# A streaming encoder on one core: layer B's q, k and v of three chunks by seven half-size products (Strassen's scheme) for eight

## Chip, core and metric

The kernel runs on one core of one Trainium2 chip. The metric is the device time of the execution in microseconds; the time before is the median of three runs. TensorE, VectorE, ScalarE and GpSimd work side by side, each through its own queue in order; SyncE issues most of the DMAs.

## What is computed

A two-layer trunk over 2048 tokens of width 1024, all in float32. The part that the change touches is layer B's input: from the stream x after layer A, the shared keys and values and the queries.

```python
kv_in = rms_norm(x, kv_norm)
k_all, v_all = jnp.split(kv_in @ w_kv, 2, axis=-1)
k_sh = rms_norm(split_heads(k_all), k_norm)
v_sh = split_heads(v_all)
h = rms_norm(x, b_norm[j])
q, z = jnp.split(h @ b_w_in[j], 2, axis=-1)
q = rms_norm(split_heads(q), b_q_norm[j])
o = stick_breaking_attention(q, k_sh, v_sh)
```

So q, k and v are each a product of (tokens x 1024) with (1024 x 1024), a row scale 1/rms per token, and for q and k a norm per head of 64.

## The kernel before

**Stages.** The tokens are cut into four chunks of 512 (`s`, 0 to 3). A first program part runs per chunk 22 steps: four pairs z and u of layer A's input (`run_z`, `run_u`), four of its output projection (`run_o`), four of the gated embedding (`run_g`, b = 0 to 3), and six of q, k, v (`run_kvq`, two column halves b of 512 for each kind). Then a second part sweeps the attention over all chunks, with layer B's z, output projection and embedding interleaved. That second part is not touched.

**Precision.** Every float32 operand of a matmul is split into a rounded high part and the remainder (a "pair", `[P, 2, 512]`), and a product is three matmuls: high x high, low x high, high x low. The high part is written by ScalarE (`split` L215, `load_w` L106 or with a gain L112), the low part, the difference, by VectorE or GpSimd (L216, L108, L113).

**The step q, k, v.** `run_kvq` (L526) takes token blocks j of 128 in pairs (`j0` 0 and 2); for each, eight blocks kt of the contraction times three matmuls into two PSUM banks (L536: token block stationary, 512 weight columns moving). That makes 2 x 2 x 8 x 2 x 3 = 192 matmuls a kind and 576 a chunk. `token_major` scales the bank by the row scale on ScalarE (L617 for q, k; L579 for v). For q and k, `keyed` squares (L619), reduces (L621), takes the root by two GpSimd operations (L79, L80), `normed` multiplies (L629), and `finish` transposes four tiles on TensorE (L638) and stores the pair to DRAM (`qd`, `kd`). For v, the rows are shifted by one token by DMA, subtracted on GpSimd (L609), halved and stored (`vd`).

**Weights.** `load_w` brings a block of 128 x 512 into `raw` (pools `io`, 10 buffers shared with other uses, and `wraw`, 3), and makes the pair in `wpair`, twelve buffers in two pools. The main loop at the end calls the load of step i + 1 ahead of the run of step i. A q, k or v step needs eight such blocks, 48 a chunk, each used for both `j0`. Weights of the second part are halved once and stored (`keep`), one or two per step in steps 8 to 21.

**Order.** The program is recorded in the order of the code, and a scheduler then places instructions on each engine, so an engine's row of instructions mixes several steps. What it made of both programs is shown under the change.

**Buffers named below.** PSUM: six banks `psd` for products (four and two, `dense()`), two `pst` for transposes. SBUF: `act`, 18 pairs (x, m, x1, x2); `t2` with tags `tmp` (8), `qn` (5), `ub` and `us` (2 each, of `run_u`'s pooling), `t4` (3).

**The embedding stage.** `run_g(s, b)` makes two tiles o = 2b and 2b + 1 of the stream: sigmoid (L506), multiply (L508), add (L509), halve into x2 (L215, L216), and a running sum of squares `acc` (L521, L524) which gives the row scale r2.

## Time and profile before

| | us |
|---|---|
| runs: median (lowest, highest) | 2769.08 (2768.56, 2769.49) |
| profiled execution: span of its instructions | 2765.4 |
| q, k, v stage of chunk 0, 1, 2, 3 | 143.2, 143.2, 143.7, 139.4 |
| embedding stage (four steps) of chunk 1, 2, 3 | 54.8, 56.5, 55.9 |

The profile gives the profiled execution's span, from its first to its last instruction; of time around the span it shows none, and the runs' median lies 3.7 us above it. A stage here is the stretch from its first matmul to the next stage's first. In a row of a group, the numbers after the bar are the time in which the group was busy, the mean ns of one instruction, and the idle time of the engine just ahead of them with what ended it. A matmul's own duration overlaps with the next one's; its pitch is read from a run of many. "128x512" is partitions x elements.

### The profile page before, as it was taken

Reading aid. Unit: us, or ns where it says so; the run is one execution under the profiler, and the core shown is the slowest. Engines: PE = TensorE matmul, PEld = TensorE weight load, DVE = VectorE, ACT = ScalarE, POOL = GpSimd, SP = SyncE. Lnnn points to the kernel's source line nnn. Section 1 sums busy time; section 2 is a strip of 40 time slices with the busy share of each in tenths; the row PEclk is TensorE's granted clock in tenths of the full one; section 3 lists DMA queues with packets and bytes.
Section 4 is the critical chain, followed back from the end, with each engine's and each line's share of the span. In section 5 each row is a group of like instructions: output and inputs, shape, how many; then the busy total and the mean of one; then the engine's idle time right before and its main releaser. Section 6 shows DMA issues by size and latency. Waiting matters only on the chain. (4 is left out here: it accounts for less than half of the span.)

```text
span 2765.4 us, 39537 instructions
## 1 busy us (share of the span) xinstructions
PE 2725.7 (99%) x13715; PEld 2260.4 (82%) x13715; DVE 1956.0 (71%) x2573; ACT 1385.5 (50%) x2801; POOL 873.7 (32%) x695
## 2 busy tenths in 40 slices
PE   9999999999999999999999999999999999999999
PEld 7888888888888888888888888887887778888877
DVE  6766535655357544565499999999999988996632
ACT  5444532445234542345356566666666655664521
POOL 2574338642475325753121111111110011112220
PEclk9999999999999999999999999999999999999999
DMA  8664696747946479445678565555555566668765
GB/s 293 236 196 171 218 325 204 225 148 253 347 148 227 163 249 318 136 145 170 191 254 278 180 217 170 169 161 178 169 159 162 159 200 200 188 204 264 249 209 160
DMA packets 335835, 573.21 MB, mean 207 GB/s; under 512 B 32462, under 2 KB 166638, under 8 KB 335636
## 3 DMA queue, kind: packets, MB, share of 16 engines
q1 hardware_dynamic: 330186, 563.03, 63.5%
q10 hardware_dynamic: 5450, 7.66, 0.9%
q8 instruction: 108, 1.77, 0.3%
q14 instruction: 91, 0.75, 0.1%
HBM read 430.01 MB, written 132.19 MB: 203 GB/s over the span
## 5 line engine op out<-in xcount | busy, mean ns | idle before, releaser
L844 ACT CAST at<-psa 128x512 fp32r<-128x512 f32 (+3 forms) x640 | 334.1, 522 | 478.4 <-PE psa L841 459.6
L536 PE MATMUL psd<-wpair,x 128*128 128x512 f32 x2304 | 544.0, 393 | 0.0
L828 DVE TENSOR_TENSOR_SCAN pp<-kap,pp,zeros 128x512 f32<-128x512 f32 x384 | 512.9, 1336 | 3.1 <-ACT kap L820 2.4
L536 PEld LDWEIGHTS psd<-wpair,x 128*128 128x128 f32 x2304 | 428.2, 188 | 86.2
L845 DVE TENSOR_TENSOR at<-psa,at 128x512 fp32r<-128x512 f32 (+3 forms) x640 | 381.0, 596 | 88.0 <-ACT at L844 84.9
L841 PE MATMUL psa<-ident,pp 128*128 128x128 f32 x2176 | 347.0, 275 | 17.2 <-DVE at L845 15.5
L820 ACT ACTIVATE kap<-psl 128x512 f32<-128x512 f32 (+3 forms) x640 | 344.9, 539 | 15.1 <-PE psl L817 12.0
L841 PEld LDWEIGHTS psa<-ident,pp 128*128 128x128 f32 x2176 | 262.9, 140 | 93.0 <-DVE at L845 38.8
L816 PE MATMUL psl<-kk,qa 128*128 128x512 f32 (+3 forms) x640 | 281.4, 440 | 0.0
L854 PE MATMUL pso<-at,vv 128*128 128x512 f32 (+3 forms) x640 | 235.1, 367 | 0.0
L817 PE MATMUL psl<-kk,qb 128*128 128x512 f32 (+3 forms) x640 | 233.0, 364 | 0.0
L853 PE MATMUL pso<-at,vv 128*128 128x512 f32 (+3 forms) x640 | 232.7, 364 | 0.0
L825 DVE TENSOR_TENSOR_SCAN pp<-kap,ahead 128x128 f32<-128x128 f32 (+3 forms) x256 | 219.8, 859 | 5.8 <-ACT kap L820 4.1
L131 PE MATMUL psd<-xp,wpair 128*128 128x512 f32 x512 | 201.9, 395 | 1.3 <-ACT xp L269 0.8
L132 PE MATMUL psd<-xp,wpair 128*128 128x512 f32 x512 | 200.5, 392 | 0.0
L133 PE MATMUL psd<-xp,wpair 128*128 128x512 f32 x512 | 200.1, 391 | 0.0
L113 DVE SCALAR_TENSOR_TENSOR wpair<-wraw,gains,wpair 128x512 fp32r<-128x512 f32 x192 | 169.7, 905 | 36.8 <-ACT wpair L112 36.1
L923 POOL TENSOR_TENSOR zr<-zr,sgz 128x512 f32<-128x512 f32 x32 | 58.8, 1836 | 368.2 <-ACT sgz L922 311.3
L112 ACT ACTIVATE wpair<-wraw,gains 128x512 fp32r<-128x512 f32 x192 | 135.0, 720 | 59.0 <-PE psd L536 32.3
L108 POOL TENSOR_TENSOR wpair<-wraw,wpair 128x512 fp32r<-128x512 f32 x99 | 145.5, 1485 | 59.7 <-ACT wpair L106 59.7
L853 PEld LDWEIGHTS pso<-at,vv 128*128 128x128 f32 x640 | 120.2, 188 | 26.9 <-ACT at L844 0.2
L854 PEld LDWEIGHTS pso<-at,vv 128*128 128x128 f32 x640 | 120.3, 188 | 25.9
(211 smaller groups left out, 5402.4 us busy)
## 6 DMA issues: line engine op xcount, KB each, us to landing
kk<-kd SPq DMA_DIRECT2D x320, 128.0 KB
vv<-vd SPq DMA_DIRECT2D x160, 256.0 KB
wraw<-in_w_kv_dram SPq DMA_DIRECT2D x128, 256.0 KB
wpair<-wzd SPq DMA_DIRECT2D x64, 512.0 KB
wpair<-wod SPq DMA_DIRECT2D x64, 512.0 KB
wpair<-wgd SPq DMA_DIRECT2D x64, 512.0 KB
wpair<-wu SPq DMA_DIRECT2D x48, 512.0 KB
wpair<-wi SPq DMA_DIRECT2D x36, 512.0 KB
```

Of the source, the lines that this page charges most:

```text
L131: T.matmul(ps, wst(units, kt, 0, c0), acts[kt][:, 0], start=(begin and kt == order[0]), stop=False)
L536: T.matmul(pss2[i], ck["x2"][kt][:, xh, tk], wst(ws, kt, wh, 0, W5), start=(kt == 0 and xh == 0 and wh == 0), stop=(kt == KT - 1 and wh == 1))
L816: T.matmul(ps[:, :w], qa[:, qs], kk[:, :w], start=True, stop=False)
L817: T.matmul(ps[:, :w], qb[:, qs], kk[:, :w], start=False, stop=True)
L820: A.activation(out=kp[:, r0:], in_=ps[:, :w], func=AF.Sigmoid, scale=-1.0)
L825: V.tensor_tensor_scan(out=pp[:, r0:][:, ::-1], data0=kp[:, r0:][:, ::-1], data1=ahead[:, r0:][:, ::-1], initial=1.0, op0=ALU.mult, op1=AL ...
L828: V.tensor_tensor_scan(out=pp[:, ::-1], data0=kp[:, ::-1], data1=zeros.to_broadcast([P, W5]), initial=st["carry"][j], op0=ALU.mult, op1=AL ...
L841: T.transpose(pt[:, j * P : (j + 1) * P], pp[:, r0 + kt * P : r0 + (kt + 1) * P], ident)
L844: A.copy(out=at[:, 0, cs], in_=pt[:, cs])
L845: V.tensor_tensor(out=at[:, 1, cs], in0=pt[:, cs], in1=f(at[:, 0, cs]), op=ALU.subtract)
L853: T.matmul(po[:, cs], vv[:, kt, :], at[:, 0, cs], start=(st["diag"] and kt == 0), stop=False)
L854: T.matmul(po[:, cs], vv[:, kt, :], at[:, 1, cs], start=False, stop=(st["last"] and kt == 3))
```

## The change

For chunks 1 to 3 (chunk 0 stays with `run_kvq`), the 1024 x 1024 product of each kind is cut into halves of the contraction (x2 tiles 0 to 3 and 4 to 7), of the tokens (256 each) and of the columns (512 each), and computed with seven products of half-size blocks and sums (Winograd's form of Strassen's scheme). With token and contraction halves A11, A12, A21, A22 of the stream and B11 to B22 of the weights:

- S1 = A21 + A22, S2 = S1 - A11 (tile `sum12`, its pair `s12`); S3 = A11 - A21, S4 = A12 - S2 (`sum34`, `s34`); made in `run_g`, b = 2 and 3, by half-width adds on GpSimd or VectorE and halved into eight more pairs
- T1 = B12 - B11, T2 = B22 - T1, T3 = B22 - B12, T4 = B21 - T2; made once by `combine`, twelve calls (three kinds, four blocks each) in chunk 0's q, k, v steps and chunk 1's steps 10 to 15, and stored in DRAM (`wtd`)
- the seven steps of a kind, in order, with the PSUM pair that each accumulates in: "11" (b), "21" (a), 2 (b, onto 11), 1 (c), 3 (b, onto 2), 4 (b, onto 3), "22" (c, onto 1). Each is 4 x 2 x 3 = 24 matmuls. Between them ScalarE copies out p1 (b after 11, tag `ub`), u2 (b after 2, tag `us`) and u3 (b after 3, tag `ub`), and VectorE adds them to what is in a or c; block 4's sum is copied by ScalarE

A step loads four weight blocks, 28 a kind and 84 a chunk; those of 1, 2, 3 and 4 come from `wtd` and need no gain. Loads run two steps ahead within these steps. The row scale goes into the square and the norm instead of a separate scaling. Transposes and stores go by pairs of token blocks. The next chunk's x is brought in and transposed in v's steps alone. The stored weights of the second part are spread otherwise over the steps.

```diff
+    def load_block(pools, src, base, gain, kind, block):
...
+            if block in (1, 2, 3, 4):
+                nc.sync.dma_start(out=raw, in_=wtd[kind, block, k])
+                A.copy(out=pr[:, 0, 0], in_=raw)
+                state["w"] += 1
+                (G if state["w"] % 2 else V).tensor_tensor(out=pr[:, 1, 0], in0=raw, in1=f(pr[:, 0, 0]),
+                                                           op=ALU.subtract)
+            else:
...
+                A.activation(out=pr[:, 0, 0], in_=raw, func=AF.Identity, scale=g)
+                V.scalar_tensor_tensor(out=pr[:, 1, 0], in0=raw, scalar=g, in1=f(pr[:, 0, 0]),
+                                       op0=ALU.mult, op1=ALU.subtract)
...
+            if b == 3:
+                u, v = held.pop()
+                halves("s12", u, V)
+            for k, t in zip((2 * b - 4, 2 * b - 3), ts):
+                lo = ck["t"][k]
+                eng = G if b == 2 else V
+                if k == 3:
+                    halves("s34", v, G)
+                    v = held.pop()
+                u = t2.tile([P, W5], F32, tag="ub", name="sum12", bufs=2)
+                w = t2.tile([P, W5], F32, tag="us", name="sum34", bufs=2)
+                eng.tensor_tensor(out=u[:, :H], in0=lo[:, H:], in1=t[:, H:], op=ALU.add)
+                eng.tensor_tensor(out=u[:, H:], in0=u[:, :H], in1=lo[:, :H], op=ALU.subtract)
+                G.tensor_tensor(out=w[:, :H], in0=lo[:, :H], in1=lo[:, H:], op=ALU.subtract)
+                G.tensor_tensor(out=w[:, H:], in0=t[:, :H], in1=u[:, H:], op=ALU.subtract)
...
+        def run_seven(s, kind, block, ws):
...
+            left, bank, c0 = {
+                "11": (x2[:4], "b", 0), "21": (x2[4:], "a", 0), 2: (s12, "b", 2 * P), 1: (s12, "c", 0),
+                3: (s34, "b", 0), 4: (x2[4:], "b", 2 * P), "22": (s34, "c", 2 * P)}[block]
+            begin = block in ("11", "21", 1)
+            if begin:
+                ck[bank] = [dense(), dense()]
+            pss2 = ck[bank]
+            for k in range(4):
+                for i in range(2):
+                    tk = slice(c0 + i * P, c0 + (i + 1) * P)
+                    for xh, wh in ((0, 0), (1, 0), (0, 1)):
+                        T.matmul(pss2[i], left[k][:, xh, tk], ws[k][:, wh, 0, :],
...
+            def kept(tag, nm, j0):
...
+                    t = t2.tile([P, W5], F32, tag=tag, name=nm, bufs=2)
...
+                        A.copy(out=t, in_=pss2[i])
...
+            if block == "11":
+                ck["p1"] = kept("ub", "p1", 0)
+            elif block == "21":
+                final(ck["a"], ck["p1"], 0, 0)
+            elif block == 2:
+                ck["u2"] = kept("us", "u2", 0)
+            elif block == 3:
+                final(ck["c"], kept("ub", "u3", 2), 1, 2)
+            elif block == 4:
+                final(ck["b"], None, 0, 2)
+            elif block == "22":
+                final(ck["c"], ck["u2"], 1, 0)
...
+            s, step = (0, i) if i < 22 else divmod(i - 22 + 37, 37)
+            ahead_of = 3 if s and step >= 15 else 2
```

**Where instructions stand, first place: VectorE where chunk 2's embedding stage ends and its q begins.** `sg2`, `tx2`, `x2` are the last two tiles of the embedding, `wpair` weight blocks. Before:

```order
L508 TENSOR_TENSOR sg2_8586<-psd_8524,sg2_8586 128x512
L508 TENSOR_TENSOR sg2_8587<-psd_8525,sg2_8587 128x512
L509 TENSOR_TENSOR tx2_8518<-sg2_8586,tx2_8518 128x512
L509 TENSOR_TENSOR tx2_8520<-sg2_8587,tx2_8520 128x512
L113 SCALAR_TENSOR_TENSOR wpair_8633<-wraw_8634,gains_101,wpair_8633 128x512
L216 TENSOR_TENSOR x2_8595<-tx2_8518,x2_8595 128x512
L216 TENSOR_TENSOR x2_8600<-tx2_8520,x2_8600 128x512
L621 TENSOR_REDUCE ssq_8722<-sqq_8720 128x8
```

After the change, from the same four instructions (sg2, sg2, tx2, tx2) on:

```order
L583 TENSOR_TENSOR sum12_9043<-tx2_8663,tx2_8946 128x256
L140 TENSOR_TENSOR wpair_9097<-wraw_9098,wpair_9097 128x512
L247 TENSOR_TENSOR x2_9023<-tx2_8946,x2_9023 128x512
L247 TENSOR_TENSOR x2_9028<-tx2_8948,x2_9028 128x512
L584 TENSOR_TENSOR sum12_9043<-sum12_9043,tx2_8663 128x256
L247 TENSOR_TENSOR s12_9040<-sum12_8894,s12_9040 128x512
L247 TENSOR_TENSOR s12_9049<-sum12_9043,s12_9049 128x512
L583 TENSOR_TENSOR sum12_9055<-tx2_8665,tx2_8948 128x256
L140 TENSOR_TENSOR wpair_9137<-wraw_9138,wpair_9137 128x512
L584 TENSOR_TENSOR sum12_9055<-sum12_9055,tx2_8665 128x256
L140 TENSOR_TENSOR wpair_9147<-wraw_9148,wpair_9147 128x512
L247 TENSOR_TENSOR s12_9061<-sum12_9055,s12_9061 128x512
```

Three instructions between tx2 and the next stage's work have become twelve.

**Second place: ScalarE in the same stretch, somewhat later.** `p1` is the copy of block 11's banks. Before:

```order
L215 CAST x2_8595<-tx2_8518 128x512
L521 ACTIVATE sq_8604<-tx2_8518 128x512
L215 CAST x2_8600<-tx2_8520 128x512
L521 ACTIVATE sq_8608<-tx2_8520 128x512
L548 COPY ss2_8713<-pst_8708 128x4
L617 ACTIVATE qs_8718<-psd_8658,r2all_103 128x512
```

After:

```order
L246 CAST s34_9052<-sum34_8895 128x512
L138 CAST wpair_9137<-wraw_9138 128x512
L682 COPY p1_9128<-psd_9102 128x512
L138 CAST wpair_9142<-wraw_9143 128x512
L138 CAST wpair_9147<-wraw_9148 128x512
L246 CAST s12_9061<-sum12_9055 128x512
L246 CAST s34_9064<-sum34_9044 128x512
L246 CAST s34_9067<-sum34_9056 128x512
L682 COPY p1_9130<-psd_9103 128x512
L138 CAST wpair_9218<-wraw_9219 128x512
```

The two p1 copies now stand among the halving of the sums, and the second waits for VectorE to be done with sum12_9055, whose buffer it takes.

**Third place: TensorE from block 3 to block 4 of chunk 2's q** (banks 9102 and 9103 are b; 9586 is the bank of k's block 11). Before, two token pairs of q follow each other in different banks:

```order
L536 MATMUL psd_8658<-wpair_8513,x2_8600 128x512 x3
L536 MATMUL psd_8659<-wpair_8513,x2_8600 128x512 x3
L545 MATMUL pst_8708<-ones_65,acc_8610 128x1 x4
L536 MATMUL psd_8742<-wpair_8478,x2_8195 128x512 x3
L536 MATMUL psd_8743<-wpair_8478,x2_8195 128x512 x3
```

After:

```order
L663 MATMUL psd_9102<-wpair_9233,s34_9067 128x512 x3
L663 MATMUL psd_9103<-wpair_9233,s34_9067 128x512 x3
L663 MATMUL psd_9586<-wpair_9410,x2_8617 128x512
L663 MATMUL psd_9102<-wpair_9266,x2_8865 128x512 x3
L663 MATMUL psd_9103<-wpair_9266,x2_8865 128x512 x3
```

Block 4 follows block 3 in the same two banks, with one matmul of another product between them.

## Prediction

> **What bounds the kernel now.** I read the page first, then the busy time of the engines stage by stage, then the matmul pitch, then the groups of the engines that feed TensorE.

> ```profile
> span 2765.4 us, 39537 instructions
> PE 2725.7 (99%) x13715; PEld 2260.4 (82%) x13715; DVE 1956.0 (71%) x2573; ACT 1385.5 (50%) x2801; POOL 873.7 (32%) x695
> PEclk9999999999999999999999999999999999999999
> ```

> TensorE is busy for 99% of the span at full granted clock, so time leaves the kernel only where matmuls leave it, or where the clock or the pitch changes. The stages that the change touches, by their stretches (the q, k, v stages of chunks 1, 2 and 3, and the gated-embedding stage before chunk 2's):

> ```profile
> core 0: us, PE busy (x) PEld busy (x) DVE busy (x) ACT busy (x) POOL busy (x), PEclk, DMA share, GB/s
> 563.30:706.50 143.20, 143.16 (x682) 118.69 (x681) 71.97 (x110) 75.35 (x149) 49.05 (x44) 1.00 0.63 209
> 837.80:894.30 56.50, 55.42 (x246) 45.33 (x245) 42.73 (x47) 29.15 (x55) 33.82 (x22) 1.00 0.73 244
> 894.30:1038.00 143.70, 143.38 (x682) 118.58 (x681) 72.62 (x106) 72.97 (x141) 49.17 (x44) 1.00 0.63 207
> 1225.40:1364.80 139.40, 139.36 (x651) 115.49 (x649) 65.73 (x95) 62.79 (x101) 44.32 (x40) 1.00 0.50 164
> ```

> In all three q, k, v stages TensorE never pauses, while VectorE and ScalarE are half idle and the DMA engines a third idle. That idle half is what the change spends. One unbroken run of these matmuls gives the pitch:

> ```profile
> 1351.75 13.08 PE L536 MATMUL psd<-wpair,x 128*128 128x512 f32 x57
> ```

> 13.08 us for 57 is 0.2295 us each.

> **The change, part by part.**

> *Matmuls removed.* A chunk has 576 of them now and 7 x 24 x 3 = 504 afterwards, 72 fewer in each of three chunks. 216 x 0.2295 = **-49.6 us**. Transposes are as many as before (only paired otherwise), so nothing else leaves TensorE. [...]

> *The start of each Strassen stage.* Here a wait is added. The first product (block 11) accumulates in the banks psd_9102 and psd_9103; block 21 follows in others; then block 2 accumulates onto the first banks again, so p1, the copy of the first product, must have been taken out. The two p1 tiles take the two "ub" buffers, and these hold the last two operand sums, sum12_9043 and sum12_9055. The second p1 copy therefore stands on ScalarE behind VectorE's s12_9061, the sixteenth VectorE instruction that is left when the embedding stage's matmuls end. VectorE's speed there, and TensorE's:

> ```profile
> 894.09 1.27 DVE L508 TENSOR_TENSOR sg<-psd,sg 128x512 f32<-128x512 f32 x2
> 895.29 1.28 DVE L509 TENSOR_TENSOR tx<-sg,tx 128x512 f32<-128x512 f32 x2
> 894.33 9.00 PE L536 MATMUL psd<-wpair,x 128*128 128x512 f32 x39
> L113 DVE SCALAR_TENSOR_TENSOR wpair<-wraw,gains,wpair 128x512 fp32r<-128x512 f32 x12 | 15.8, 1338 | 1.7 <-ACT wpair L112 1.7
> L216 DVE TENSOR_TENSOR x<-tx,x 128x512 fp32r<-128x512 f32 x8 | 9.6, 1234 | 0.0
> L509 DVE TENSOR_TENSOR tx<-sg,tx 128x512 f32<-128x512 f32 x8 | 6.2, 818 | 0.0
> L508 DVE TENSOR_TENSOR sg<-psd,sg 128x512 f32<-128x512 f32 x8 | 5.1, 679 | 0.0
> L108 DVE TENSOR_TENSOR wpair<-wraw,wpair 128x512 fp32r<-128x512 f32 x4 | 4.5, 1125 | 6.5 <-ACT wpair L106 6.5
> L211 ACT COPY rbx<-pst 128x512 f32<-128x512 f32 x3 | 1.7, 579 | 0.0
> ```

> The first three rows are of the time around 894.33, where the stage starts; the next five are means over 837.8 to 907. VectorE work with both sources in SBUF is slow there because GpSimd works at the same time: the halving of a weight takes 1.338 against 0.773 in the stage after it (row below), the one from PSUM stays at 0.679. From 894.33, VectorE has the two sg behind it at +1.0; two tx (0.82) +2.7; then, in the order of the changed program, half-width sum (half of 1.23) +3.3; weight 1.13 +4.4; two x2 +6.9; sum +7.5; two s12 +10.0; sum +10.6; weight +11.7; sum +12.3; weight +13.5; s12_9061 +14.7; and the p1 copy (0.58) +15.3. TensorE reaches psd_9103 after 51 matmuls, +11.7. It waits 3.6 us; what stands behind it on TensorE is everything, on ScalarE behind the copy the weights of block 3, which have 11 us. Bounds: if GpSimd left VectorE alone (0.64 for each as in the first two rows, 0.77 for a weight, half of that for a sum), s12_9061 is done at +9 and nothing waits; if all its two-source work took 1.34, at +17.1, and the wait is 6.0. I take 3.6, since GpSimd gets twelve half-width adds, two halvings and weights just there: **+10.8 us** for three chunks (0 to 18).

> *Bank taken twice in a row.* Block 4 accumulates onto the banks of block 3, from which u3 has just to be copied; in q and k one matmul of the next product stands between, in v of chunks 1 and 2 transposes. The last product on the first bank starts 0.92 us before block 4 could, takes 0.39, so the copy can run from -0.5 to +0.1; half of another ScalarE instruction (0.72, row below) ahead of it makes +0.4. Nine times about 0.5: **+4.5 us** (0 if the filler covers it; 14 if two instructions stand ahead).

> *Feeding the products.* A chunk loads 84 weight blocks for 48. Order and rows, per chunk:

> ```profile
> L113 DVE SCALAR_TENSOR_TENSOR wpair<-wraw,gains,wpair 128x512 fp32r<-128x512 f32 x37 | 27.8, 773 | 6.0 <-ACT wpair L112 6.0
> L112 ACT ACTIVATE wpair<-wraw,gains 128x512 fp32r<-128x512 f32 x37 | 26.0, 720 | 9.0 <-PE psd L536 7.3 <-PE psd L133 1.5 <-DMA kd<-hl 0.2
> L629 DVE TENSOR_TENSOR qn<-qs,rq 128x512 f32<-128x512 f32 x16 | 11.0, 690 | 11.8 <-POOL rq L80 11.7
> DMA packets 17582, 29.92 MB, mean 209 GB/s; under 512 B 1564, under 2 KB 9500, under 8 KB 17572
> ```

> (of 563.3 to 706.5.) VectorE had 72 us of work there. In the changed program's stage it has 23 differences of combined weights (x 1.125 = 25.9), 18 evictions from PSUM (x 0.68 = 12.2), sums and their halves (about 6), and nine fewer weights with gain (-7.0): 109 us in a stage of about 132. ScalarE: 75.4, and 45 casts of weights (at most 0.72, so 28 to 32) for nine weights with gain (-6.5), and some ten more casts of sums and stored weights (6): about 105. DMA: 0.63 x 143.2 = 90 us for 29.9 MB, and 42 more loads of 0.26 MB make about 33 more: 123. All three fit beside TensorE, with two blocks (11 us) of weights ahead as cushion, so this would cost nothing; but three in-order queues at 80 to 93% do not mesh perfectly, and I take 1.5 us a chunk, **+4.5 us** (0 to 42; the upper end is the second rival).

> *Made once.* The twelve combinations stand beside chunk 0's q, k, v, whose VectorE and GpSimd are as idle as chunk 1's above (hidden), and beside chunk 1's output and embedding stages. There each adds two VectorE and two GpSimd operations, and with the sums GpSimd goes from 34 of 56 us to about 55: the start of chunk 1's stage then comes later. **+3 us** (0 to 8). Moving the stored halves of other weights (the "kept" loads) from chunk 3 into chunks 1 and 2's stages is within the 123 and 105 above. The entry into attention gets v's heads 0 to 7 later by some 16 us (three blocks less follow them), but their first use is eight steps in: nothing (0 to 8).

> Sum: -49.6 + 10.8 + 4.5 + 4.5 + 3.0 = -26.8. The profiled span of 2765.4 becomes 2738.6; the runs shown lie 3.7 us above the span (median 2769.08), which I carry: **2742.3 us**.

> **The rivals.**

> *Everything hides.* If the p1 copies come in time and the bank copies fit under the filler, the gain is nearly whole: 2769.1 - 49.6 + 3 = 2722 to 2730. For it speaks that VectorE's two pairs at 894 ran at 0.64 even with GpSimd's weights just before; against it that GpSimd will now be busy without a break there.

> *VectorE becomes the bound* (the other side). The 109 us take VectorE's undisturbed durations. If GpSimd's 22 new differences slow all two-source work as in the embedding stage, 28 weights cost 0.565 more and 16 norms perhaps 0.4 more: 131. VectorE also waits now 11.8 us for GpSimd's rq (row of qn); with GpSimd at twice the work, 23.6: 155, less the cushion of eight weights (9): 146 against 143.2 in chunks 1 and 2; chunk 3 has 65.7 now, so 139 against 139.4. It decides when VectorE's work and waits pass 152 us a stage; with two or three more waits of the same kind (+4 a chunk) the whole is 2769 + 3 + 3 + 0 + 12 = 2787. A part of the way gives 2758 to 2772.

> *The clock drops in the pause.* At the start of the program the matmuls ran at 0.43 us until 11 us, then at 0.23:

> ```profile
> 8.82 0.63 PE L133 MATMUL psd<-xp,wpair 128*128 128x512 f32 x1
> 9.25 0.63 PE L132 MATMUL psd<-xp,wpair 128*128 128x512 f32 x1
> 11.20 0.40 PE L132 MATMUL psd<-xp,wpair 128*128 128x512 f32 x1
> 11.44 0.39 PE L133 MATMUL psd<-xp,wpair 128*128 128x512 f32 x1
> PE psao L986 <- DVE sg L980: 7.2, 4, 2.4
> 2762.00:2765.40 3.40, 0.00 (x0) 0.00 (x0) 0.00 (x0) 0.12 (x1) 0.00 (x0) 0.52 0.27 77
> ```

> and once TensorE had ended, the clock was granted at 0.52. From the first dense matmul (7.4) to full speed took 3.6 us, at about half pace, so a pause that lowers the clock costs 1.8 more, 5.4 for three: 2748. No pause inside the span lowered it, but the longest that TensorE spent on one wait was 2.4 us (the row of its waits, last number). [...]

> **How the numbers follow.** Forecast (three pauses, small leaks, 2730 to 2757) 0.52; everything hides 0.14; the clock drops 0.07; a late entry into attention or a backlog from chunk 1's combinations, 2750 or so, 0.05; VectorE bound 0.22, of which 0.05 ends below 2763, 0.08 within 0.2% of 2769 and 0.09 above. 0.2% (5.5 us) is about what a measurement of this kernel can tell from no change. So faster 0.83, same 0.08, slower 0.09. The range goes from 2722 (everything hides) to 2772, which leaves out some 0.05 below and 0.10 above.

> **What would show it.** Right: in the three stages 504 matmuls at 0.2295, one pause of 3 to 4 us in TensorE 11 to 16 us after each stage's start, released by ScalarE's p1 copy, and stages of about 131 us (127 in chunk 3). Wrong, if that pause is absent and the stage takes 127 us; if the pauses lie evenly over q and k and end with weights from VectorE (the bound moved); if granted clock falls below 1.00 after the pause; or if other stages grow.

## The result, and the profile after

| | before | after |
|---|---|---|
| median of 4 runs, us | 2768.82 (2768.47 to 2769.49) | 2916.38 (2914.14 to 2921.65) |
| profiled execution, us | span 2765.4 | span 2919.9, time 2921.65 |

The ratio is 1.0536, 95% interval 1.0521 to 1.0551: the change makes the kernel 148 us slower. 2742.3 was forecast, and the range ended at 2772.

The head of the page after, to be read against the three lines of before: span, busy time of the engines, granted clock in 40 slices.

```profile
span 2919.9 us, 40205 instructions
PE 2740.6 (94%) x13499; PEld 2256.2 (77%) x13499; DVE 2115.6 (72%) x2711; ACT 1480.6 (51%) x2957; POOL 1063.5 (36%) x839
PEclk9999999989999999999999999999999999999999
```

The 216 matmuls are gone (13715 to 13499), and still TensorE is busy 14.9 us longer. Its idle time (span less busy) went from 39.7 to 179.3 us: 139.6 of the 154.5 us are pauses. The rest is pace: 14.9 us more busy time with 49.6 us of matmuls removed means that the others took 64.5 us more. Most of that is the clock: in the stretches in which it was halved TensorE was busy for 111.7 us in all. Matmuls of 512 columns started 0.43 us apart there (1257.82 to 1260.38, clock 0.50) and 0.23 us apart at full clock (1261.37 to 1264.32), so about half of the 111.7, some 56 us by estimate, is lost pace. The rest of the 64.5 was not traced.

The stages of after: q, k, v of chunk 0; then in turn what lies between two such stages and the q, k, v of chunks 1, 2 and 3. The first number behind the stretch is its length, the next TensorE's busy time.

```profile
core 0: us, PE busy (x) PEld busy (x) DVE busy (x) ACT busy (x) POOL busy (x), PEclk, DMA share, GB/s
236.20:396.00 159.80, 146.31 (x681) 119.13 (x680) 75.67 (x114) 80.93 (x142) 58.96 (x50) 0.99 0.67 221
396.00:600.90 204.90, 193.72 (x829) 157.93 (x828) 116.39 (x130) 76.68 (x135) 133.58 (x109) 0.97 0.76 255
600.90:779.20 178.30, 138.73 (x609) 111.92 (x608) 125.69 (x152) 100.60 (x197) 104.50 (x85) 0.89 0.73 241
779.20:974.50 195.30, 189.64 (x829) 156.31 (x829) 109.24 (x128) 68.19 (x129) 130.05 (x107) 0.98 0.76 250
974.50:1149.00 174.50, 144.95 (x609) 115.79 (x609) 116.62 (x144) 97.00 (x189) 94.35 (x79) 0.88 0.68 219
1149.00:1348.50 199.50, 191.27 (x830) 157.08 (x828) 106.63 (x128) 69.20 (x129) 132.66 (x109) 0.97 0.69 224
1348.50:1509.80 161.30, 135.82 (x580) 109.63 (x579) 107.78 (x131) 83.88 (x142) 87.20 (x71) 0.89 0.59 187
```

Before, the three stages of the seven products took 143.2, 143.7 and 139.4 us with TensorE never idle; now 178.3, 174.5 and 161.3 at a mean clock of 0.89. Chunk 0's stage, whose matmuls did not change, takes 159.8. The stretches between, 204.9, 195.3 and 199.5, were these:

```profile
376.90:563.30 186.40, 186.40 (x830) 154.42 (x830) 103.80 (x122) 66.65 (x124) 122.72 (x99) 1.00 0.73 241
706.30:894.30 188.00, 186.92 (x829) 154.27 (x828) 104.83 (x124) 65.44 (x123) 121.36 (x98) 1.00 0.70 235
1037.90:1225.40 187.50, 186.95 (x830) 154.28 (x829) 106.64 (x120) 65.21 (x122) 118.99 (x95) 1.00 0.65 211
```

What TensorE waited for in chunk 2's stage of after (total us, times, longest one):

```profile
PE pst L800 <- DVE qn L790: 7.7, 5, 2.2
PE pst L800 <- DVE hl L812: 6.0, 1, 6.0
PE psd L663 <- ACT p L682: 6.0, 2, 4.7
PE psd L663 <- ACT u L680: 5.3, 2, 3.3
PE psd L663 <- DVE wpair L147: 3.1, 1, 3.1
```

The two longest items are the transposes of q and k (L800). One such pair of tiles, in time; start, duration, and in brackets the wait and its releaser:

```profile
1037.25 0.68 DVE L700 TENSOR_TENSOR qs<-psd,u 128x512 f32<-128x512 f32 x1
1039.28 1.30 POOL L140 TENSOR_TENSOR wpair<-wraw,wpair 128x512 fp32r<-128x512 f32 x1 [2.50 <-ACT wpair L138]
1041.26 1.64 POOL L83 TENSOR_TENSOR rq<-ms,neghalf 128x8 f32<-128x8 f32 x1
1042.93 0.75 DVE L790 SCALAR_TENSOR_TENSOR qn<-qs,r2all,rq 128x512 f32<-128x512 f32 x1 [1.22 <-POOL rq L83]
1043.83 1.64 POOL L83 TENSOR_TENSOR rq<-ms,neghalf 128x8 f32<-128x8 f32 x1
1045.50 1.74 DVE L790 SCALAR_TENSOR_TENSOR qn<-qs,r2all,rq 128x512 f32<-128x512 f32 x1 [1.81 <-POOL rq L83]
1047.76 1.40 DVE L812 SCALAR_TENSOR_TENSOR hl<-pst,gqk,hl 128x512 fp32r<-128x512 f32 x2
1048.56 1.12 PE L800 MATMUL pst<-ident,qn 128*128 128x128 f32 x4 [6.00 <-DVE hl L812]
```

From the eviction (qs, 1037.25) to the end of the second qn (1047.24) it takes 10.0 us: a weight's difference stands on GpSimd ahead of the mean and root, the two roots follow each other there, and VectorE waits in order for each. The eviction hl of the transposes before stands on VectorE behind both qn, so their bank comes free only then. TensorE reaches these transposes one block of 24 matmuls (5.5 us) after the products.

The clock around that pause, in stretches of 3.4 us (last three columns: granted clock, DMA share, GB/s):

```profile
1042.10:1045.50 3.40, 0.46 (x2) 0.03 (x1) 0.75 (x1) 1.46 (x3) 3.23 (x4) 1.00 0.41 131
1045.50:1048.90 3.40, 0.34 (x2) 0.35 (x3) 3.40 (x4) 0.00 (x0) 1.19 (x1) 0.50 0.24 76
1048.90:1052.30 3.40, 3.40 (x13) 2.91 (x12) 1.61 (x3) 1.19 (x2) 1.27 (x1) 0.50 0.92 310
1052.30:1055.70 3.40, 3.40 (x16) 2.81 (x16) 1.96 (x3) 2.49 (x6) 0.58 (x2) 1.00 0.92 293
```

The pause of 6 us halves the clock for two stretches, and the second of them is full of work at half pace.

### The profile page after: what moved, and what is told of

Its sections match the earlier page's. It is cut to its first block, busy times and chain, and to the rows that moved or that the text cites. A ratio compares the mean times of both kernels' runs of the same rounds, so it can differ in the third digit from the quotient of the medians.

```text
span 2919.9 us, 40205 instructions
## 1 busy us (share of the span) xinstructions
PE 2740.6 (94%) x13499; PEld 2256.2 (77%) x13499; DVE 2115.6 (72%) x2711; ACT 1480.6 (51%) x2957; POOL 1063.5 (36%) x839
## 5 line engine op out<-in xcount | busy, mean ns | idle before, releaser
L1057 PE MATMUL psa<-ident,pp 128*128 128x128 f32 x2176 | 346.9, 274 | 18.1 <-DVE at L1061 16.5
L1036 ACT ACTIVATE kap<-psl 128x512 f32<-128x512 f32 (+3 forms) x640 | 345.0, 539 | 15.0 <-PE psl L1033 11.8
L663 PE MATMUL psd<-wpair,s 128*128 128x512 f32 x864 | 222.2, 416 | 17.6 <-ACT p L682 13.3
L663 PEld LDWEIGHTS psd<-wpair,s 128*128 128x128 f32 x864 | 172.9, 203 | 56.2 <-ACT p L682 14.5
L663 PE MATMUL psd<-wpair,x 128*128 128x512 f32 x648 | 170.6, 418 | 20.3 <-DVE wpair L147 6.0
L663 PEld LDWEIGHTS psd<-wpair,x 128*128 128x128 f32 x648 | 128.2, 203 | 52.2 <-DVE wpair L147 6.9
```

The source lines that it names most:

```text
L663: T.matmul(pss2[i], left[k][:, xh, tk], ws[k][:, wh, 0, :], start=(begin and k == 0 and xh == 0 and wh == 0), stop=(k == 3 and wh == 1), s ...
L1036: A.activation(out=kp[:, r0:], in_=ps[:, :w], func=AF.Sigmoid, scale=-1.0)
L1057: T.transpose(pt[:, j * P : (j + 1) * P], pp[:, r0 + kt * P : r0 + (kt + 1) * P], ident)
```

## The experiments

Theory A: latency. The transposes stand too close behind the norm's chain, engines in order wait for GpSimd's root, and each pause halves the clock. Rival B: throughput; VectorE and GpSimd are full of weight halving. C: the wait for p1 is what counts. E came after the first four runs: ScalarE stands in order behind the combinations' fetches. Each kernel was measured beside the kernel before, whose median was 2767.7 to 2769.3 us each time.

### Transposes one block later (late)

```diff
-            if block in ("11", 1, 4):
-                while lag:
-                    lag.pop(0)()
+            ripe, lag[:] = lag[:], []
+            for fn in ripe:
+                fn()
...
-                for fin in fins:
-                    fin()
+                if kind == "v":
+                    for fin in fins:
+                        fin()
+                else:
+                    pend.extend(fins)
...
+            for fin in pend:
+                fin()
+            pend.clear()
```

Each block now ends with the transposes that became ready one block ago, and the multiplications (`pend`) of the final before it. The small tiles `ssq` and `rq` get five buffers each for it.

> The changed kernel (2916.4 us) with each norm's multiplication and each pair of transposes of q and k, in chunks 1 to 3, one block of 24 matmuls (5.5 us) later than in the change; nothing is added or left out. Theory A (latency: the transposes stand too close behind the norm chain, VectorE waits in order for GpSimd's rq, and each pause halves the clock): the waits named qn and hl in the three stages, 55 us, and most of the 45 or so that the halved clock cost there go: 2800 to 2840 us. Rival B (throughput: the halving of weights fills VectorE and GpSimd, and the waits only show where they fall behind): under 20 us go, 2895 to 2916 us.

2891.59 us (ratio to before 1.0453, 1.0438 to 1.0469): 24.8 us less. Between the two theories. In chunk 2 the transposes' wait on hl is gone, that on qn is not:

```profile
PE pst L808 <- DVE qn L798: 9.3, 4, 3.1
```

### Own buffers for p1 and u3 (own)

```diff
-                ck["p1"] = kept("ub", "p1", 0)
+                ck["p1"] = kept("p1", "p1", 0)
...
-                final(ck["c"], kept("ub", "u3", 2), 1, 2)
+                final(ck["c"], kept("p1", "u3", 2), 1, 2)
```

> The changed kernel (2916.4 us) with p1 and u3 in two buffers of their own, no longer in those of sum12; two start-up tiles share another tag to make room. Theory A takes this as a separate pause: the wait for the copy p1 goes from each of three stages (6 us each, measured) with the clock lost behind it (about 3 us each): 2885 to 2900 us. Rival B: the wait moves to the next product, 2910 to 2920 us. What was predicted for this wait alone, 3.6 us for each stage: 2905 us.

2920.35 us (1.0551, 1.0535 to 1.0566): no gain. The wait for p1 left chunk 2's stage and came back at the transposes, whose qn rose from 7.7 to:

```profile
PE pst L800 <- DVE qn L790: 15.3, 6, 6.8
```

The wait was real, but the time it took was lost again a little later, in waits for VectorE's qn.

### Combined weights stored as halves (halved)

```diff
+            if block in (1, 2, 3, 4):
+                nc.sync.dma_start(out=f(pr), in_=wtd[kind, block, k])
+                continue
...
+                pr = t2.tile([P, 2, 1, W5], F32R, tag="t4", name="cpair", bufs=3)
+                split(pr[:, :, 0], u, V)
+                nc.sync.dma_start(out=wtd[kind, t, k], in_=f(pr))
```

> The changed kernel (2916.4 us) with the combined weights kept as two halves that have been split once, when they are made; so blocks 1 to 4 take no casts and no differences (16 casts on ScalarE and 8 differences on each of VectorE and GpSimd less for each of q, k, v in a chunk), and 4.2 MB more are loaded for each of them in a chunk, less what the whole blocks took. Theory A: GpSimd's norm chain loses the weight difference that stands between its two halves, so some of the waits for qn shrink, 2870 to 2905 us. Rival B (throughput of VectorE and GpSimd): all waits of the stages of chunks 1 to 3 go, 2800 to 2840 us. A third possibility, that the loads bind: slower, 2930 us or more.

2986.58 us (1.078, 1.0761 to 1.08): in the range of the third possibility, but not shown to be for its reason. The time is lost up to the end of chunk 1's stage (230.5 us for 178.3), after the combinations, which now carry the splitting too: from 600 us to that stage's end SyncE's queue waits 62.0 us for their halves before it can store them, and in the stage TensorE waits 25.0 us for stored halves to be fetched and 21.6 once for ScalarE. The later stages fell, chunk 2's from 174.5 to 158.4 us and chunk 3's from 161.3 to 141.0, the latter with VectorE at 74.9 us instead of 107.8, so the halving has a part in the stages of the products.

### The combinations alone (combos, noact, nofetch, nowork, spaced)

The kernel before, with the twelve combinations and nothing that uses them:

```diff
+            if s == 0 and step >= 16 or s == 1 and 10 <= step < 16:
+                combos.pop(0)()
```

> The kernel before (2768.8 us) with the twelve combinations of weights made and stored at the same steps as in the change, and nothing that uses them. As predicted for them: 0 to 8 us, 2769 to 2777 us. Rival: the combinations are what makes the changed kernel's chunk 0 (16.8 us longer) and the front of its chunk 1 (18 us longer) long: 2795 to 2805 us.

2819.46 us (1.0187, 1.0172 to 1.0203): 51.7 us, where 3 had been forecast. ScalarE waits for the fetched rows (craw), and TensorE in the stretch between chunk 0's and chunk 1's stages for ScalarE's casts of x:

```profile
ACT craw L711 <- DMA craw<-in_w_kv_dram: 44.9, 10, 11.0
PE psd L134 <- ACT x L218: 10.2, 2, 6.9
```

Without the scaling on ScalarE (`A.activation(out=raw, in_=raw, func=AF.Identity, scale=g)` left out):

> The kernel before with the combinations alone (2819.5 us against 2767.7), without their scaling by the gains on ScalarE; nothing uses them, so the result is the reference's. Theory E (ScalarE waits in order for the rows of a combination, and the casts of x stand behind it): nearly all goes, 2769 to 2785 us. Rival: GpSimd or VectorE standing in order behind the fetch, or the transfers themselves, cost as much: 2800 to 2820 us.

2805.72 us (1.0132, 1.0115 to 1.0149). ScalarE's part is some 14 us; the rival has the rest.

The work and the stores without the fetches (scaled from a tile that stays), and the fetches and the stores without the work, each as an edit against combos:

```diff
-                nc.sync.dma_start(out=raw.rearrange("q e n -> q (e n)"), in_=src[row * P : (row + 1) * P, base : base + D])
+                for e in range(2):
+                    A.activation(out=raw[:, e], in_=resident, func=AF.Identity, scale=g)
```

> The kernel before with the combinations alone (2819.5 us against 2767.7), scaled from one tile that stays on the chip instead of from fetched rows: the same scaling, sums, differences and stores, no fetch; what is stored is meaningless and unused, so the result is the reference's. If engines waiting in order for a fetch are what costs: 2768 to 2785 us. If it is the work itself: 2805 to 2820 us.

```diff
-                A.activation(out=raw, in_=raw, func=AF.Identity, scale=g)
...
-            G.tensor_tensor(out=t3, in0=b22, in1=b12, op=ALU.subtract)
...
-            for t, u in ((3, t3), (1, b12), (2, t2_), (4, b21)):
+            for t, u in ((3, b11), (1, b12), (2, b22), (4, b21)):
```

> The kernel before with the fetches and stores of the combinations alone, nothing scaled or combined; the result is the reference's. If traffic, or the load queue standing behind a fetch's buffer, is what costs: 2800 to 2820 us. If engines waiting for the fetch or the work itself: 2768 to 2778 us.

2810.50 us (1.0147, 1.013 to 1.0164) and 2800.72 us (1.0112, 1.0097 to 1.0127). The work with the stores costs 41 us, the fetches with the stores 31, all together 52; the stores are in both. Neither is the single cause, and as 41 are left without any fetch, waiting for fetched rows alone (theory E) is not it. In the run without the work TensorE waited for weights that were fetched late:

```profile
PE psd L134 <- DMA wpair<-wi: 10.6, 1, 10.6
```

With each fetch a whole step ahead of its use (`fetch` loads the four rows' halves, `make` is the rest):

```diff
+        places = ([((0, 7 + 2 * i), (0, 8 + 2 * i)) for i in range(7)] + [((0, 21), (1, 0))]
+                  + [((1, 7 + 2 * i), (1, 8 + 2 * i)) for i in range(3)] + [((1, 12), (1, 13))])
+        for (fetch, make), (one, two) in zip(combos, places):
+            aside.setdefault(one, []).append(fetch)
+            aside.setdefault(two, []).insert(0, make)
```

> The kernel before with the combinations alone (2819.5 us against 2767.7), where the rows of a combination are fetched a whole step (11 us or more) before they are used, behind no store of the combination before, one combination in two steps for most; the same work and bytes. Theory E (what costs is engines that stand in order behind a fetch that comes late): 2768 to 2785 us. Rival (the work on VectorE, GpSimd and ScalarE, some 7 us of each engine in a combination, falls on the path wherever it is put): 2800 to 2820 us.

2828.92 us (1.0215, 1.0198 to 1.0232). Not better than combos, but the edit did not do what it was made for: ScalarE still waited 79.0 us for rows (54.2 in combos), and the combinations also stand at other steps. So it shows only that an earlier fetch in the program does not heal it, as in the changed kernel below; against theory E itself speaks the run without fetches.

### Fetches a step ahead in the changed kernel (ahead)

```diff
-            aside[0, 16 + i] = combos[i : i + 1]
-            aside[1, 10 + i] = aside[1, 10 + i] + combos[6 + i : 7 + i]
+            for s, step, (fetch, make) in ((0, 16 + i, combos[i]), (1, 8 + i, combos[6 + i])):
+                aside.setdefault((s, step), []).insert(0, make)
+                aside.setdefault((s, step - 1), []).append(fetch)
```

> The changed kernel (2916.4 us), with the weight rows of each combination fetched one step before they are scaled and combined, into the buffers of sum12 and sum34 instead of those of the transposed q and k; the six combinations of chunk 1 stand two steps earlier. The same work is done. Theory E, formed on the run with the combinations alone (2819.5 us against 2767.7, ScalarE waiting 11.0 us in order for a fetch that was issued in the same step): nearly all of that goes, 40 to 50 us: 2866 to 2880 us. Rival: it is the combinations' own work and stores that cost, 2900 to 2916 us.

2931.57 us (1.0584, 1.0566 to 1.0601): slower, and ScalarE waits no less for the rows of k and v (49.7 us; 45.8 in the change itself). The fetch is earlier in the program, but shares SyncE's queue with loads that wait for buffers (40.0 us for those of weights, the longest 11.9) and stores that wait for results (23.0 us for GpSimd's). So the waits that the edit was to remove stayed, and it says little on theory E.

### No differences of combined weights on GpSimd (gfree)

```diff
-                (G if state["w"] % 2 else V).tensor_tensor(out=pr[:, 1, 0], in0=raw, in1=f(pr[:, 0, 0]),
-                                                           op=ALU.subtract)
+                V.tensor_tensor(out=pr[:, 1, 0], in0=raw, in1=f(pr[:, 0, 0]), op=ALU.subtract)
```

> The changed kernel (2916.4 us) with the differences of the combined weights all on VectorE; in the change every second one is on GpSimd, in front of or between the norm's mean and root. Theory A (latency through GpSimd): the waits for qn and for the eviction hl behind it shrink, 2880 to 2905 us. Rival B (VectorE is what is full, 116.6 us busy in a stage of 174.5): with 24 more differences on it in each chunk it falls further behind, 2920 to 2960 us.

2892.30 us (1.0448, 1.0433 to 1.0464): 24.1 us less, in theory A's range. In chunk 2 TensorE's waits for qn and hl fell from 13.7 to 8.6 us. Groups of VectorE in chunk 2's stage (count, then busy us and mean ns, then idle time before them); first after, then this run:

```profile
L140 DVE TENSOR_TENSOR wpair<-wraw,wpair 128x512 fp32r<-128x512 f32 x23 | 21.4, 949 | 8.7 <-ACT wpair L138 8.7
L790 DVE SCALAR_TENSOR_TENSOR qn<-qs,r2all,rq 128x512 f32<-128x512 f32 x16 | 18.0, 1127 | 24.2 <-POOL rq L83 24.0
```

```profile
L139 DVE TENSOR_TENSOR wpair<-wraw,wpair 128x512 fp32r<-128x512 f32 x47 | 35.4, 788 | 10.8 <-ACT wpair L138 10.8
L788 DVE SCALAR_TENSOR_TENSOR qn<-qs,r2all,rq 128x512 f32<-128x512 f32 x16 | 12.0, 751 | 22.3 <-POOL rq L83 22.1
```

VectorE does 24 more differences in hardly more time (117.4 us busy against 116.6), since its instructions with both sources in SBUF are faster with GpSimd busy for 62.4 us instead of 94.4: qn takes 751 ns for 1127, a difference 788 for 949. The reduction ssq, with one source, stays (680 for 678). VectorE's own wait for rq hardly shrank (24.0 to 22.1 us), so the gain can come from the faster VectorE as well as from the shorter way through GpSimd; the run does not separate them.

### Transposes at a short distance in the kernel before (pairs5, pairs11)

```diff
-                    while j0 == 0 and kt == KT - 1 and lag:
+                    while kt == KT // 2 - 1 and lag:
```

(pairs11: `while kt == KT - 1 and lag:`; both with the pairing of the change.)

> The kernel before (2768.8 us) with the transposes of q and k made for each pair of token tiles, 24 matmuls (5.5 us) behind the pair's eviction, as the change has them after two of its four finished pairs; nothing else of the change. Theory A in its pure form (the chain eviction, square, sum, mean and root on GpSimd, multiplication for two tiles takes 6 us or more whatever else runs): each of 32 places waits 1 to 2.5 us and some of them halve the clock, 2820 to 2890 us. Rival: at the load of before the chain is done in time or nearly, and it is the change's further work on VectorE and GpSimd that stretches it, 2769 to 2790 us.

> The kernel before (2768.8 us) with paired transposes 48 matmuls (11 us) behind the pair's eviction, twice the distance of the run that took 2824.1 us. Theory A (a chain of 6 to 8 us at this load): the waits are gone, 2766 to 2776 us. Rival: the pairing itself costs (twice as many, smaller stores; two banks in a row for the transposes), in each stage about as in the change's chunk 0: 2790 to 2825 us.

2824.08 us (1.0201, 1.0186 to 1.0216) and 2767.25 us (0.9996, 0.9987 to 1.0006). Pairing is free; the distance costs 55 us, in a kernel whose VectorE is half idle. One pair in pairs5, and TensorE's waits in that stage:

```profile
604.55 0.69 ACT L617 ACTIVATE qs<-psd,r2all 128x512 f32<-128x512 f32 x1
606.99 1.64 POOL L80 TENSOR_TENSOR rq<-ms,neghalf 128x8 f32<-128x8 f32 x1
609.50 1.64 POOL L80 TENSOR_TENSOR rq<-ms,neghalf 128x8 f32<-128x8 f32 x1
611.17 0.69 DVE L629 TENSOR_TENSOR qn<-qs,rq 128x512 f32<-128x512 f32 x1 [1.81 <-POOL rq L80]
```

```profile
PE pst L638 <- DVE qn L629: 11.9, 9, 1.6
```

The chain takes 7.3 us (604.55 to 611.86) with no more work beside it than the kernel before has, and TensorE comes after 5.5. The clock holds nearly through all four stages (1.00, 0.99, 1.00 and 0.99); two of them:

```profile
234.10:390.50 156.40, 144.50 (x682) 118.18 (x680) 75.73 (x115) 77.62 (x153) 49.69 (x44) 1.00 0.63 201
576.80:734.80 158.00, 146.12 (x681) 119.58 (x680) 74.61 (x110) 76.83 (x150) 51.74 (x45) 0.99 0.61 195
```

### No combinations; several edits at once (nocombo, free, freeown, freehalf, best, best2)

nocombo leaves the combinations out of the changed kernel, and blocks 1 to 4 fetch an uncombined quarter:

```diff
-                nc.sync.dma_start(out=raw, in_=wtd[kind, block, k])
+                nc.sync.dma_start(out=raw, in_=src[k * P : (k + 1) * P, base + W5 : base + D])
```

> The changed kernel (2916.4 us) without the making of the combined weights; blocks 1 to 4 fetch an uncombined quarter of the same size in their place, so the result is not the reference's, and all later work and traffic is the same. If the combinations cost here what they cost alone in the kernel before (51.7 us): 2860 to 2870 us. Rival: in the change the pauses that they make are filled or shared with others, 2885 to 2916 us. As predicted for them (3 us): 2908 to 2916 us.

2884.19 us (1.041, 1.0395 to 1.0426): 32.2 us less, just past the rival's edge; so of the 51.7 some 20 seem to share pauses with the rest. Chunk 0's stage and the stretch behind it are back near their lengths of before (143.2 and 186.4):

```profile
234.90:381.30 146.40, 143.32 (x681) 118.24 (x680) 71.81 (x108) 72.67 (x141) 45.40 (x41) 1.00 0.58 184
381.30:568.60 187.30, 186.96 (x830) 154.26 (x829) 100.79 (x119) 64.17 (x119) 121.68 (x101) 1.00 0.68 225
```

free is nocombo with the edits of late and gfree:

> The same as the run without the combinations, and with the transposes one block later (25 us alone) and the combined weights' differences all on VectorE (24 us alone). The result is not the reference's. If the three causes add up: 2916 less 50, 25 and 24, 2810 to 2825 us, so that over 60 us of what the change adds stay unexplained. If the causes named are all that holds the gain back: 2725 to 2765 us.

2823.34 us (1.0196, 1.0181 to 1.0211): the three together give 93.0 us, a little more than their sum (32.2 + 24.8 + 24.1 = 81.1). The largest wait left in chunk 2's stage is p1's:

```profile
PE psd L663 <- ACT p L682: 4.7, 2, 3.6
```

freeown is free with p1 and u3 in own buffers:

> The run without combinations, with later transposes and all differences on VectorE (2823.3 us), and p1 and u3 in buffers of their own. No combined weights are made, so the result is not the reference's. Theory C (the wait for p1 is real, but hidden behind other pauses as long as these stand): its 5 to 7 us in each of three stages go and so do the 10 us at half clock behind each: 2790 to 2800 us. Rival (the pause moves to the next product, as it did in the changed kernel): 2815 to 2825 us.

2821.16 us (1.0186, 1.0171 to 1.0201): the rival again. p1's wait goes, qn's grows from 2.2 to 7.2:

```profile
PE pst L806 <- DVE qn L796: 7.2, 6, 2.8
```

freehalf is freeown with ready halves of other weights in blocks 1 to 4, nothing cast or subtracted for them:

```diff
+            if block in (1, 2, 3, 4):
+                nc.sync.dma_start(out=f(pr).rearrange("q e o n -> q (e o n)"),
+                                  in_=list(split_once.values())[k].rearrange("q e k n -> q (e k n)"))
+                continue
```

> The run freeown (2821.2 us: no combinations, later transposes, differences on VectorE, own buffers for p1 and u3), with blocks 1 to 4 fetching ready halves of another weight, twice the bytes, so that nothing is cast or subtracted for them; the result is not the reference's. Rival B, the load of VectorE and ScalarE (some 112 and 95 us busy in a stage): the stages of the seven products fall from 155, 151 and 131 us to 127 to 135 each, 2765 to 2790 us. If the fetches into the pairs come late, as in the run halved: 2800 to 2850 us.

2826.12 us (1.0196, 1.0175 to 1.0216; single runs from 2815.01 to 2828.07, the profiled span 2813.2). The stages of the seven products, first freeown, then freehalf:

```profile
568.40:723.60 155.20, 136.65 (x609) 109.99 (x608) 113.40 (x167) 94.91 (x189) 61.89 (x54) 0.93 0.75 242
919.90:1071.20 151.30, 135.21 (x610) 109.44 (x609) 111.70 (x167) 94.68 (x189) 60.37 (x53) 0.94 0.77 248
1276.40:1407.60 131.20, 125.75 (x581) 103.17 (x580) 104.39 (x154) 82.34 (x142) 54.63 (x47) 0.99 0.71 227
```

```profile
567.30:713.90 146.60, 131.69 (x609) 105.31 (x608) 81.57 (x121) 72.93 (x145) 57.92 (x55) 0.99 0.93 325
915.90:1064.40 148.50, 134.16 (x610) 107.44 (x609) 82.59 (x121) 72.90 (x145) 57.51 (x56) 0.97 0.93 320
1270.40:1398.30 127.90, 125.09 (x577) 102.60 (x575) 74.50 (x108) 58.76 (x97) 51.20 (x47) 0.99 0.90 311
```

This profile is of the fastest run, 11 us below the median, which itself is no better than freeown's. In it the stages fall by 14.7 us in all, and only chunk 3's reaches the 127 to 135: in chunk 2 TensorE waits for the fetches instead (10.6 us of waits, the longest 4.7), with the DMA engines at 0.93. Most of what VectorE gave back, the fetches took.

best is the changed kernel with late, gfree and ahead; best2 has the spaced fetches and p1's own buffers in place of ahead. Nothing is left out in either:

> The changed kernel (2916.4 us) with three edits at once: transposes and multiplications one block later (2891.6 us alone), the combinations' rows fetched a step ahead, the combined weights' differences all on VectorE. If the three causes are apart and add up: 2916 less 25, less 40 to 50, less 10 to 30, 2810 to 2845 us; still slower than before. If they share their pauses: 2850 to 2880 us.

> The changed kernel with all four edits: transposes and multiplications one block later, the combined weights' differences all on VectorE, p1 and u3 in own buffers, combinations fetched a whole step ahead. If theories C and E hold: 2795 to 2815 us. If C falls: 2823 to 2840 us; if E falls: 2840 to 2860 us. None of these beats the kernel before (2768.8 us).

2869.85 us (1.0365, 1.0349 to 1.038) and 2863.60 us (1.0343, 1.0327 to 1.0358). Chunk 3's stage takes 131.0 us in best2, less than before's 139.4; the rest keeps the loss.

## Why the prediction was wrong, point by point

- **Matmuls removed, -49.6: right.** 13499 are left, and in the stage that runs most freely (freehalf, chunk 3) TensorE is busy for 125.1 us against 139.4 before: 14.3 less, where a third of the term is 16.5. The gain is there, and is buried.
- **"Transposes are as many as before (only paired otherwise), so nothing else leaves TensorE": this step failed.** The count was right and the distance was not looked at. The change brings two of its four finished pairs to one block, 5.5 us, behind their products. The chain that they wait for takes 7.3 us at the load of the kernel before (pairs5) and 10.0 in the changed kernel. pairs5 and pairs11 show this alone: 55 us or nothing. The change has 12 such pairs (two each for q and k in three chunks) where pairs5 has 32; in proportion that is 21 of the 55, an estimate, and in the change late gives back 24.8. The prediction asked of the bank copies when they would be late, and not of the transposes.
- **Combinations made once, +3 (0 to 8), "hidden": this step failed too.** 51.7 us alone, 32.2 within the change. They were costed by the idle share of VectorE and GpSimd, but TensorE paused for work of these engines and of ScalarE that came late: in combos 10.2 us for ScalarE's casts of x, in the change 10.2 us for the last halves of x at the start of chunk 1's stage, which are gone in nocombo. The work with the stores costs 41, the fetches with the stores 31. Where each microsecond goes was not separated further.
- **Feeding, 1.5 us a chunk.** The loads were forecast fairly well: VectorE 109 us (measured 125.7, 116.6 and 107.8 in the three stages), ScalarE about 105 (100.6, 97.0, 83.9), DMA 123 (0.68 x 174.5 = 119 in chunk 2). The conclusion, that what fits hides, did not follow. The mechanism of the second rival was at work (qn at 1127 ns for 690, 24.0 us of waits for rq, forecast as 23.6), but its price of 2787 was much too low: it counted these as more work for VectorE, and not as delay on the way to the transposes. Moving GpSimd's differences to VectorE gave back 24.1 us, with qn at 751 ns instead of 1127 (gfree).
- **p1, +10.8.** The waits are there, 1.1, 6.0 and 6.2 us in the three stages, 13.3 together; two of them reach the upper bound of 6.0. But as a cost the term was zero or nearly: removing it changed nothing twice (own, freeown), since the time went to the next wait in line.
- **Bank taken twice, +4.5:** before block 4's products TensorE waited 0.7, 3.3 and 0 us in the three stages, 4.0 together. The size is right, the place by half: the waits are in v of chunks 1 and 2 alone, none in q and k. Another 4.3 us went to waits for u2 before block 3 (2.3 and 2.0, also in v), which the sum did not have.
- **The clock rival** (0.07, one 1.8 us loss a stage) was right as a mechanism and far too small: the clock fell not three times but 27 times within the span, and some 56 us were lost to half pace.
- **Entry into attention, nothing (0 to 8):** from chunk 3's last product to the end of the span it was 1400.6 us, and is 1410.1, so +9.5.

**What stays open.** free still lies 54.8 us over the kernel before and 81 over the forecast. Its stages of the seven products take 157.4, 152.0 and 133.3 us against 131, 131 and 127 forecast, 53.7 of the 81. (These three figures leave out part of the sum's small terms; with all of them they would be 133, 134 and 130, and the excess 46.) The remainder is elsewhere: against the kernel before, free is longer by 4.9 us ahead of chunk 1's stage, 8.4 and 14.9 in the two stretches between the stages (202.4 us ahead of chunk 3's, against 187.5) and 12.4 from chunk 3's last product to the end. halved's later stages and freehalf's profile show that part of the excess in the stages is the halving of the weights, and freehalf's median that less halving by more traffic is no way out. The stored halves of other weights that the change moved (the kept loads), and the sums' own work on GpSimd, were not tried alone; they are suspected for the remainder and not shown. No version found beats the kernel before; the fastest that has the seven products and leaves nothing out is best2, 3.4% slower.

## What to carry to other kernels

When a change shortens the work between a producer and its consumer, count the microseconds between them on the engine that sets the end, and compare them with the whole latency of the chain, engine by engine, with and without the further work of the change beside it; equal counts of instructions say nothing. Idle shares did not hide work in these in-order queues: with VectorE busy for two thirds of a stage here (116.6 of 174.5 us in chunk 2), TensorE paused for a sixth of it (29.55 us), and the combinations, put beside a stage at "half idle", cost ten times their estimate (32.2 us for 3, within the change). Taking away one long wait (p1's) showed little while the next one stood right behind it (own 2920.35 us for 2916.38, freeown 2821.16 for 2823.34), so test waits together before calling one of them free.
